# Latent attention in a two-layer decoder trunk: queries and keys of a head left on the partitions of their product, and pair projections kept apart

## The chip, the core and the metric

The kernel runs on one core of one Trainium2 chip. The metric is the device time of one execution in microseconds (us). Five engines matter: TensorE (PE, matmuls; PEld is its weight load), VectorE (DVE), ScalarE (ACT), GpSimd (POOL), and SyncE (SP), whose queue issues every DMA of this kernel. Matmuls write into PSUM, from where only ACT and DVE read the results; SBUF holds everything else, on 128 partitions.

## The reference

Two layers, each with four gated branches on the same input (512 positions, 1024 channels): RWKV-7 time mixing, multi-head latent attention, a causal depthwise convolution of width 31, and cross-attention into 256 memory tokens. The branches are projected, merged by gates, projected once more, and normalised. The change lies in latent attention, with 8 heads, 64 dimensions without and 32 with rotation:

```python
def _mla_branch(q_lat, kv_lat, k_pe, gate, cos, sin, q_norm, w_uq, kv_norm, w_ukv):
    q = (_rms_norm(q_lat, q_norm) @ w_uq).reshape(B, S, H, MLA_NOPE + MLA_ROPE)
    kv = (_rms_norm(kv_lat, kv_norm) @ w_ukv).reshape(B, S, H, MLA_NOPE + MLA_V)
    ...
    q_full = jnp.concatenate([q_nope, q_pe], axis=-1)
    k_full = jnp.concatenate(
        [k_nope, jnp.broadcast_to(k_pe[:, :, None, :], (B, S, H, MLA_ROPE))], axis=-1)
    o = _causal_block_attention(q_full, k_full, v, (MLA_NOPE + MLA_ROPE) ** -0.5)
    return o.reshape(B, S, BRANCH_WIDTH) * jax.nn.silu(gate)
```

A second place is RWKV's token shift, `p = p + mu * (p_prev - p)`, which mixes each position with the one before it.

## The kernel before, in words

**Precision.** Every fp32 operand of a projection is split in two parts, h (a rounded cast) and l (the rest). A product is three matmuls: h by l, h by h, l by h (`mm3`). So a projection of 128 channels by 512 positions over 1024 input channels is 24 matmuls of 128x512 (`project`).

**Order of the work.** The program is straight-line, and Python decides its order while building it. A class `Plan` (L67) keeps an estimated clock for each engine. The main stream (`stream`, L1860) yields the projections' matmuls one after another; everything else (evacuations, softmax steps, convolution taps) is a generator that was spawned as a task with a due time. `Plan.run` (L147) takes the task that is due first if its time has come on PE's clock, and otherwise the next piece of the stream. A task that yields the word "slack" is due no earlier than DVE's clock. The order so found is the order of the instructions on each engine; the waits between engines are added from the data they share.

**Weights.** `stream` works on a list of items. `pick` chooses the first item that is ready; `prefetch` starts the weight DMAs of up to four half-blocks ahead into two raw buffers; `weights` (L435) spawns the split of each, a cast on ACT and a subtraction on DVE. So at any time casts of coming weights (names like w24h) stand in ACT's queue between the evacuations.

**PSUM.** The pool "pp" has two buffers for projections, "pa" has two, "pg" has four for attention. A projection's first matmul waits until the buffer of the one before the last has been read out.

**A pair of heads.** Latent attention goes by four pairs per layer. `pair_item` (L1416) takes one block of weights, issues the DMAs that put the rotated rows of the queries (qrh, qrl) into rows 64 to 96 of the head's tiles qT and qTl, and then has 9 matmuls for the queries of two heads (pq) and 6 for their keys (pk), each into one buffer of "pp". In a product head 0 lies on partitions 0 to 64 and head 1 on 64 to 128. `heads` (L1441) evacuates it: one ACT operation writes the h part xqh or xkh, one DVE operation the l part xql or xkl, both on 128 partitions, into staging tiles; then four DMAs of half a tile each bring the heads' rows to rows 0 to 64 of qT, qTl, kTh and kTl. A head's score matmuls (`mla_block`, L1471: ms) use rows 0 to 96. After the softmax, mt transposes the probabilities and mo multiplies them with the values.

**Other work in the same stretch.** The projections xq of cross-attention (ps_xq), its scores and products (xs, xt, xo, with the transposed probabilities xPTh and xPTl), gates (ps_mg, ps_xg), and the convolution's 31 taps per channel block on DVE (cacc), which fill DVE between the rest.

Of the kernel before, what the change touches and what calls it, by code (L numbers as in the profile page):

```python
# [21 lines left out]
LAYERS = 2  # L22
SEQ = 512
DM = 1024
U_SLOTS = 32
ORDER = ["z0", "m0", "m1", "z2", "m2", "m4", "z3", "m3", "m5"]
LOOK = 4
GATHER = 1500.0
# [38 lines left out]
class Plan:  # L67
# [79 lines left out]
    def run(self, stream):  # L147

        blocked, over, last = None, False, 0.0
        while True:
            now = self.now()
            for task in self.tasks:
                if callable(task[2]) and task[2]():
                    task[0], task[2] = max(task[0], now), None
                elif task[2] == "slack":
                    task[0] = max(task[0], self.clk["DVE"])
            if self.cut != (128, 128):
                last = now  # L160
            wait = last + GATHER if self.cut == (128, 128) and not over else 0.0
            due = min((x for x in self.tasks if not callable(x[2])),
                      key=lambda x: max(x[0], wait) if x[2] == "small" else x[0], default=None)
            at = due and (max(due[0], wait) if due[2] == "small" else due[0])
            if blocked == "pe" or callable(blocked) and blocked() or isinstance(blocked, float) and blocked <= now:
                blocked = None
            if due is not None and at <= now:
                self._step(due)
            elif blocked is None and not over:
                self.t = now  # L170
                try:
                    blocked = next(stream)
                except StopIteration:
                    over = True
            else:
                times = [due[0]] if due is not None else []
                if isinstance(blocked, float):
                    times.append(blocked)
                if times:
                    last = 0.0  # L180
                    self.clk["PE"] = max(now, min(times))
# [84 lines left out]
def trunk_kernel(ctx: ExitStack, tc: tile.TileContext, A, out, dbg=None):  # L266
# [87 lines left out]
    tsh = cp.tile([128, 512], F32, tag="tsh", name="tsh")  # L354
    G.memset(tsh[:, 0:1], 0.0)
# [242 lines left out]
    def layer_items(l):  # L598
        items = []
# [3 lines left out]
        def pr(n, i=0, w=1):  # L603
            return PRM[l][0][:, PCOL[n] + i:PCOL[n] + i + w]
# [5 lines left out]
                return PRM[l][1][:, c:c + 1]  # L610
            return PRM[l][0][:, PCOL[n] + i:PCOL[n] + i + 1]

        def item(blocks, run, ready=None, picked=None, soon=None):
            items.append((blocks, run, ready, picked, soon))

        def ch_item(i, name, after, ready=None, picked=None):

# [62 lines left out]
            plan.spawn(parts())  # L680

        def mix(i, ps, dst):
            S.activation(tsh[:, 1:512], ps[:, 0:511], AF.Copy, scale=pr("mu", i))
            V.scalar_tensor_tensor(out=dst, in0=ps, scalar=PRM[l][2][:, i:i + 1], in1=tsh, op0=ALU.mult, op1=ALU.add)

        def wlal(ps):
            x = u("lora" + t_)
# [435 lines left out]
        def taps(i, hpad):  # L1123
            a = u(f"cacc{i}" + t_)
            V.tensor_scalar(out=a, in0=hpad[:, 0:512], scalar1=hp("conv_w", 31 * i), scalar2=pr("conv_b", i), op0=ALU.mult, op1=ALU.add)
            yield
            for k in range(1, 31):
                V.scalar_tensor_tensor(out=a, in0=hpad[:, k:k + 512], scalar=hp("conv_w", 31 * i + k), in1=a, op0=ALU.mult, op1=ALU.add)
                L["taps"][i] = k
                yield "slack"  # L1130
            cacc[i] = a
            L["nacc"] += 1
            if L["nacc"] == 4:
                yield from conv_norm()

        def conv_norm():
# [18 lines left out]
            for i in range(4):  # L1155
                ps, = yield from pa.take([128, 512], f"cb{i}" + t_)
                plan.due(*ntok)
                yield "pe"
                for tb in range(4):
                    TR(ps[:, 128 * tb:128 * tb + 128], ntok[tb][:, 128 * i:128 * i + 128])  # L1160
                yield
                t, z = u(f"ctn{i}" + t_), u(f"yc{i}" + t_)
# [95 lines left out]
        def lat_item(nb):  # L1258
            def run(get):
# [14 lines left out]
                if nb == 0:  # L1274
# [7 lines left out]
                    L["kT"] = [tuple(m(f"kT{n}{i}" + t_, 512, f"kT{n}{i}", 1, 96, F32R) for n in "hl") for i in range(4)]  # L1282
# [16 lines left out]
        def key_rotary():  # L1299
# [13 lines left out]
            pa.free()  # L1313
            plan.due(*kr)
            yield
            for kT in L["kT"]:
# [77 lines left out]
        def query_rotary(qp):  # L1394
# [9 lines left out]
            for g in range(2):  # L1404
# [8 lines left out]
                pa.free()  # L1413
                qpe.append(t)

        def pair_item(hh):  # L1416
            def run(get):
                wq = yield from get()
                wk = yield from get()
                there = []  # L1420
                qT = [(m(f"qT{hh}{h}" + t_, 512, "lq", 4, 96, F32R),
                       m(f"qTl{hh}{h}" + t_, 512, "qo", 1, 96, F32R) if hh % 2 > h else
                       u(f"qTl{hh}{h}" + t_, 512, F32R, 96) if hh % 2 else m(f"qTl{hh}{h}" + t_, 512, "qp", 2, 96, F32R)) for h in range(2)]
                kT = [L["kT"][2 * (hh % 2) + h] for h in range(2)]
                for h in range(2):
                    r = 64 * (hh % 2) + 32 * h
                    for x, y in zip(qT[h], qpe[hh // 2]):
                        DMA(x[64:96].bitcast(F32), y[r:r + 32].bitcast(F32), f"qTpe{hh}{h}" + t_)
                for w, ks, T, n, s in ((wq, range(3), qT, "q", MSCALE), (wk, range(3, 5), kT, "k", 1.0)):
                    ps = pp.tile([128, 512], F32, tag="pp", name=f"p{n}{hh}" + t_)  # L1430
                    for i, k in enumerate(ks):
# [4 lines left out]
                    plan.spawn(heads(T, ps, n, s, there))  # L1436
                plan.spawn(pair(hh, qT, kT, there))
            item([(A["w_qk"][l, hh], (384, 256))], run,
                 lambda: len(latT) == 5 and len(qpe) > hh // 2 and len(vtok) == 4 and L["pairs"] >= hh - 1 and MEM[l] is not None)

        def heads(T, ps, n, s, there):  # L1441

            parts = [u(f"x{n}{x}" + t_, 512, F32R) for x in "hl"]
            S.activation(parts[0], ps, AF.Copy, scale=s)
            V.scalar_tensor_tensor(out=parts[1], in0=ps, scalar=s, in1=parts[0].bitcast(F32), op0=ALU.mult, op1=ALU.subtract)
            plan.due(*parts)
            yield
            for i, x in enumerate(parts):
                for h in range(2):
                    y = T[h][i]  # L1450
                    DMA(y[0:64].bitcast(F32), x[HALF[h]].bitcast(F32), f"{n}{i}{h}" + y.tensor.name)
                    there.append(f"{n}{i}{h}" + y.tensor.name)

        def pair(hh, qT, kT, there):
            yield lambda: L["turn"] == hh and len(there) == 8
            mo, = yield from pg.take([128, 512], f"mo{hh}" + t_)
            plan.t = max(plan.t, *(plan.done[x][0] for x in there + [f"qTpe{hh}1" + t_]))
            yield
            left = [2]
            for i in range(4):  # L1460
# [10 lines left out]
        def mla_block(hh, h, i, T, mo, two, done, left):  # L1471
# [388 lines left out]
    def stream(items):  # L1860


        items, todo, held, runs = list(items), [], [], []
        count, look = [0], [3]

        def pick():
            for n, (blocks, run, ready, _, _) in enumerate(items):
# [6 lines left out]
            for n, (blocks, run, ready, _, soon) in enumerate(items):  # L1874
                if soon and soon():
                    return n
            return None

        def prefetch():
            while len(held) < look[0] + (0 if items else 2) and wlive["raw"] < WR:  # L1880
                if not todo:
                    n = pick()
                    if n is None:
                        return
                    blocks, run, _, picked, _ = items.pop(n)
                    if picked:
                        picked()
                    todo.extend(blocks)
# [133 lines left out]
```

## Time and profile before

| | |
|---|---|
| median of 3 runs | 1520.82 us (1518.16 to 1522.56) |
| the profiled execution's own time | 1519.87 us |
| its span in the trace | 1518.1 us |
| mean granted clock of PE | 0.997 |
| PE busy | 1485.7 us, 98% |
| DVE, ACT, POOL busy | 71%, 45%, 9% |
| DMA traffic | 153.54 MB, mean 101 GB/s |

Rows of the page and of the trace name a group of instructions by line, engine, operation and tile, such as "L235 ACT ACTIVATE xqh<-pq 128x512". Line 235 is the wrapper through which all ACT, DVE and POOL operations go, 286 that of matmuls, 291 that of transposes, 298 that of DMAs, so tiles tell more than lines. "x8 | 4.8, 598" means eight instructions, 4.8 us busy in all, 598 ns each. What stands in brackets, or behind the second bar, is idle time of that engine just before, and what ended it.

### The profile page before, as it was taken

What the parts mean: (1) busy time and instruction counts of PE and PEld (TensorE: products, weight loads), DVE (VectorE), ACT (ScalarE), POOL (GpSimd) and SP (SyncE); (2) the same over time, 40 slices, a digit from 0 to 9 for tenths busy, and PEclk for the clock granted to TensorE, in tenths of its full rate; (3) what the DMA queues carried; (4) which work ended last, traced back from release to release, by engine and by line L of the source; (5) the groups of instructions that cost most, each with busy time, mean ns of one, the idle gap of its engine ahead of it and who ended that gap; (6) DMA issues with size and microseconds to landing.
All of it is one profiled execution on the core that took longest, in us unless ns stands there. A gap on an engine that the chain in (4) does not pass through costs nothing.

```text
span 1518.1 us, 29700 instructions
## 1 busy us (share of the span) xinstructions
PE 1485.7 (98%) x11896; PEld 1238.0 (82%) x11896; DVE 1072.7 (71%) x2231; ACT 686.6 (45%) x1499; POOL 135.8 (9%) x323
## 2 busy tenths in 40 slices
PE   8999999999999999999999999999999999999997
PEld 8877788887887878888999877888887878788886
DVE  5788988765757675555554889997766586756747
ACT  5535653445245453344255556533443545443432
POOL 0000000030402021000010000000030303120002
PEclk9999999999999999999999999999999999999999
DMA  6443333322232323433343252433232323235231
GB/s 211 124 113 93 104 100 98 98 85 83 74 93 60 94 74 93 139 98 114 123 146 114 81 125 69 121 107 97 81 99 61 93 64 93 69 95 181 98 116 65
DMA packets 89018, 153.54 MB, mean 101 GB/s; under 512 B 41008, under 2 KB 47152, under 8 KB 88880
## 3 DMA queue, kind: packets, MB, share of 16 engines
q1 hardware_dynamic: 88880, 151.65, 33.9%
q8 instruction: 93, 1.52, 0.4%
q14 instruction: 45, 0.37, 0.1%
HBM read 134.32 MB, written 5.77 MB: 92 GB/s over the span
## 4 chain that ended last, share of the span: by engine, by line
PE 89%; DVE 5%; DMA 2%; ACT 2%; issue 1%; SPq 1%; POOL 0%; ACTq 0%; DVEq 0%; POOLq 0%
PE ps_m L286 22%; PE po L286 11%; PE ps_cg L286 3%; PE ps_rg L286 3%; PE ps_v L286 3%; PE ps_xg L286 3%; PE ps_mg L286 3%; PE ps_k L286 3%; PE ps_r L286 3%; PE ps_val L286 3%; PE pz L286 2%; PE ms L286 2%; PE pl L286 2%; PE ps_glu L286 2%; PE ps_xq L286 2%; PE x L286 2%
## 5 line engine op out<-in xcount | busy, mean ns | idle before, releaser
L235 DVE SCALAR_TENSOR_TENSOR cacc<-hpad,prm,cacc 128x512 f32<-128x512 f32 x240 | 178.9, 748 | 3.3
L235 ACT ACTIVATE tm<-ps_m,prm 128x512 f32<-128x512 f32 x64 | 44.1, 689 | 148.5 <-PE ps_m L286 134.7
L235 DVE SCALAR_TENSOR_TENSOR mt<-tm,po 128x512 f32<-128x512 f32 x48 | 33.0, 687 | 79.2 <-PE po L286 79.1
L235 POOL TENSOR_SCALAR ZT<-W 64x256 f32<-64x256 f32 x8 | 4.8, 600 | 621.8 <-DMA W<-scr 287.7
L235 POOL TENSOR_TENSOR ZT<-ZT,tmpW 64x14 f32<-64x14 f32 (+6 forms) x112 | 44.0, 393 | 8.8
L235 ACT ACTIVATE mP<-ms,nmm 128x512 f32<-128x512 f32 (+3 forms) x64 | 33.7, 529 | 18.3 <-DVE nmm L235 17.4
L235 POOL TENSOR_TENSOR tmpW<-ZT,W 64x14 f32<-64x14 f32 (+6 forms) x112 | 39.9, 356 | 7.9
L235 ACT COPY mPT<-mt 128x512 f32<-128x512 f32 (+3 forms) x64 | 26.7, 429 | 22.4 <-PE mt L291 17.1
L235 DVE TENSOR_TENSOR merged<-merged,mt 128x512 f32<-128x512 f32 x48 | 33.8, 704 | 1.6
L235 DVE TENSOR_REDUCE nmm<-ms 128x1 f32<-128x512 f32 (+3 forms) x64 | 29.9, 483 | 0.6 <-PE ms L286 0.2
L235 POOL TENSOR_SCALAR gr<-gm 128x8 f32<-128x8 f32 x8 | 2.3, 286 | 311.2 <-DVE gm L235 311.2
L291 PE MATMUL mt<-cst,mP 128*128 128x128 f32 x160 | 27.1, 276 | 2.6 <-DVE mP L235 2.2
L235 DVE SCALAR_TENSOR_TENSOR merged<-tm,po 128x512 f32<-128x512 f32 x16 | 11.0, 687 | 22.0 <-PE po L286 20.3
L235 DVE TENSOR_SCALAR mP<-mP,smm 128x512 f32<-128x512 f32 (+3 forms) x64 | 24.8, 387 | 2.3
L235 ACT ACTIVATE yb<-yb,mr,gr 128x64 f32<-128x64 f32 x64 | 22.1, 430 | 9.0 <-DVE mr L235 9.0
L235 POOL TENSOR_SCALAR lrs<-lmv 128x1 f32<-128x1 f32 x8 | 2.5, 315 | 263.5 <-DVE lmv L235 261.8
L291 PEld LDWEIGHTS mt<-cst,mP 128*128 128x128 f32 x160 | 18.6, 141 | 8.2 <-ACT mo L235 2.2
L235 ACT ACTIVATE z<-z,lnb,lrs 128x256 f32<-128x256 f32 (+1 forms) x16 | 9.6, 647 | 31.2 <-DVE lnb L235 31.2
L286 PE MATMUL ms<-kTl,qT 96*128 96x512 f32 (+3 forms) x64 | 22.2, 347 | 0.0
L286 PE MATMUL mo<-mPT,v 128*64 128x128 f32 x320 | 21.4, 278 | 0.5 <-ACT mPT L235 0.5
L286 PE MATMUL ms<-kTh,qT 96*128 96x512 f32 (+3 forms) x64 | 20.6, 322 | 0.0
L286 PEld LDWEIGHTS mo<-mPT,v 128*64 128x64 f32 x320 | 17.3, 136 | 4.0 <-issue 2.9
(3535 smaller groups left out, 5323.2 us busy)
## 6 DMA issues: line engine op xcount, KB each, us to landing
w<-in_w_ch_dram SPq DMA_DIRECT2D x146, 512.0 KB, 3.6
w<-in_w_o_dram SPq DMA_DIRECT2D x32, 512.0 KB, 3.6
w<-in_w_out_dram SPq DMA_DIRECT2D x16, 512.0 KB, 3.6
w<-in_w_lat_dram SPq DMA_DIRECT2D x16, 336.0 KB, 3.3
w<-in_w_mk_dram SPq DMA_DIRECT2D x8, 512.0 KB, 3.5
w<-in_w_mv_dram SPq DMA_DIRECT2D x8, 512.0 KB, 3.5
w<-in_w_qk_dram SPq DMA_DIRECT2D x8, 320.0 KB, 3.1
x<-in_xT_dram SPq DMA_DIRECT2D x8, 256.0 KB, 5.6
```

The costliest lines, as they stand in the source:

```text
L235: return self.plan.keep(f(*a, **k))
L286: plan.keep(nc.tensor.matmul(o, lhsT, rhs, start=start, stop=stop))
L291: plan.keep(nc.tensor.transpose(o, i, ident))
```

## The change

- `heads` writes each half of a product straight into the head's own tile, on the partitions where the half lies: for each half one ACT operation (h part) and one DVE operation (l part) on 64 partitions, with a yield between the halves. The staging tiles and the copies by DMA are gone, 8 of 128 KB per pair, 64 in all.
- Tiles qT, qTl, kTh, kTl get 128 rows instead of 96. For head 0 of a pair nothing moves. For head 1 the product's rows are 64 to 128, the rotated ones 32 to 64, and rows 0 to 32 are set to zero by POOL; its score matmuls run over 128 rows (`ROPE`, `ROWS`).
- `pair_item` is marked `apart`: `pick` does not take a pair directly behind a pair if another item is ready.
- The convolution's taps yield "idle" instead of "slack", which makes them due one unit after DVE's clock.
- RWKV's `mix` needs no shift tile: ACT writes (1 - mu) times the product into the destination, and DVE adds mu times the product, one position on, in place. The pool of staging tiles has 33 slots instead of 32, and one tile of the convolution's normalisation moved to another pool.

In the order that this gives, layer 0 has pair 0, then a projection of xq, then pair 1 spread among scores; pair 2 is followed by scores and ps_mg, pair 3 by ps_xq. In layer 1 pair 1 comes right behind pair 0, pair 2 is followed by ps_val, and pair 3 is spread. The number of matmuls is the same, 9336 instructions in the program; ACT and DVE get 16 operations more each, POOL 23 more.

```diff
         def mix(i, ps, dst):
-            S.activation(tsh[:, 1:512], ps[:, 0:511], AF.Copy, scale=pr("mu", i))
-            V.scalar_tensor_tensor(out=dst, in0=ps, scalar=PRM[l][2][:, i:i + 1], in1=tsh, op0=ALU.mult, op1=ALU.add)
+            S.activation(dst, ps, AF.Copy, scale=PRM[l][2][:, i:i + 1])
+            V.scalar_tensor_tensor(out=dst[:, 1:512], in0=ps[:, 0:511], scalar=pr("mu", i), in1=dst[:, 1:512], op0=ALU.mult, op1=ALU.add)
...
-                yield "slack"
+                yield "idle"
...
-                    task[0] = max(task[0], self.clk["DVE"])
+                    task[0] = max(task[0], self.clk["DVE"] + (task[2] == "idle"))
...
+                    for i in (1, 3):
+                        for x in L["kT"][i]:
+                            G.memset(x[0:32].bitcast(F32), 0.0)
...
-                    DMA(x[64:96].bitcast(F32), y.bitcast(F32))
+                    DMA(x[ROPE[i % 2]].bitcast(F32), y.bitcast(F32))
...
+        ROPE, ROWS = [slice(64, 96), slice(32, 64)], [slice(0, 96), slice(0, 128)]
...
-                        DMA(x[64:96].bitcast(F32), y[r:r + 32].bitcast(F32), f"qTpe{hh}{h}" + t_)
+                        if h:
+                            G.memset(x[0:32].bitcast(F32), 0.0)
+                        DMA(x[ROPE[h]].bitcast(F32), y[r:r + 32].bitcast(F32), f"qTpe{hh}{h}" + t_)
...
-        def heads(T, ps, n, s, there):
-
-            parts = [u(f"x{n}{x}" + t_, 512, F32R) for x in "hl"]
-            S.activation(parts[0], ps, AF.Copy, scale=s)
-            V.scalar_tensor_tensor(out=parts[1], in0=ps, scalar=s, in1=parts[0].bitcast(F32), op0=ALU.mult, op1=ALU.subtract)
-            plan.due(*parts)
-            yield
-            for i, x in enumerate(parts):
-                for h in range(2):
-                    y = T[h][i]
-                    DMA(y[0:64].bitcast(F32), x[HALF[h]].bitcast(F32), f"{n}{i}{h}" + y.tensor.name)
-                    there.append(f"{n}{i}{h}" + y.tensor.name)
+        def heads(T, ps, s, there):
+
+            for half, (hi, lo) in zip(HALF, T):
+                S.activation(hi[half], ps[half], AF.Copy, scale=s)
+                V.scalar_tensor_tensor(out=lo[half], in0=ps[half], scalar=s, in1=hi.bitcast(F32)[half], op0=ALU.mult, op1=ALU.subtract)
+                there.extend((hi, lo))
+                yield
...
-            mm3(ps, *(x[:, dg] for x in T[0]), *(x[:, 0:n] for x in T[1]), True, False)
+            mm3(ps, *(x[ROWS[h], dg] for x in T[0]), *(x[ROWS[h], 0:n] for x in T[1]), True, False)
...
-                    return n
+                    if not (apart and last[0]):
+                        return n
+                    second = n if second is None else second
+            if second is not None:
+                return second
```

More of the change, by code (lines that the diff above doesn't have):

```diff
@@ L24 @@
 DM = 1024
-U_SLOTS = 32
+U_SLOTS = 33
 ORDER = ["z0", "m0", "m1", "z2", "m2", "m4", "z3", "m3", "m5"]
@@ L156, in run @@
                     task[0], task[2] = max(task[0], now), None
-                elif task[2] == "slack":
-                    task[0] = max(task[0], self.clk["DVE"])
+                elif task[2] in ("slack", "idle"):
+                    task[0] = max(task[0], self.clk["DVE"] + (task[2] == "idle"))
             if self.cut != (128, 128):
@@ L353, in trunk_kernel @@
     G.memset(mhalf, -0.5)
-    tsh = cp.tile([128, 512], F32, tag="tsh", name="tsh")
-    G.memset(tsh[:, 0:1], 0.0)
     hpads = [cp.tile([128, 542], F32, tag=f"hpad{i}", name=f"hpad{i}") for i in range(2)]
@@ L611, in hp, with item @@
             return PRM[l][0][:, PCOL[n] + i:PCOL[n] + i + 1]
-        def item(blocks, run, ready=None, picked=None, soon=None):
-            items.append((blocks, run, ready, picked, soon))
+        def item(blocks, run, ready=None, picked=None, soon=None, apart=False):
+            items.append((blocks, run, ready, picked, soon, apart))
         def ch_item(i, name, after, ready=None, picked=None):
@@ L1161, in conv_norm @@
                 yield
-                t, z = u(f"ctn{i}" + t_), u(f"yc{i}" + t_)
+                t, z = sp.tile([128, 512], F32, tag="tg", name=f"ctn{i}" + t_), u(f"yc{i}" + t_)
                 S.activation(t, ps, AF.Tanh, scale=hp("cln_g", i), bias=hp("cln_b", i))
@@ L1281, in run @@
                     L["kpe"] = m("kpe" + t_, 128, "kpe", 1)
-                    L["kT"] = [tuple(m(f"kT{n}{i}" + t_, 512, f"kT{n}{i}", 1, 96, F32R) for n in "hl") for i in range(4)]
+                    L["kT"] = [tuple(m(f"kT{n}{i}" + t_, 512, f"kT{n}{i}", 1, 128, F32R) for n in "hl") for i in range(4)]
+                    for i in (1, 3):
+                        for x in L["kT"][i]:
+                            G.memset(x[0:32].bitcast(F32), 0.0)
                 for tb in range(4):
@@ L1315, in key_rotary @@
             yield
-            for kT in L["kT"]:
+            for i, kT in enumerate(L["kT"]):
                 for x, y in zip(kT, kr):
-                    DMA(x[64:96].bitcast(F32), y.bitcast(F32))
+                    DMA(x[ROPE[i % 2]].bitcast(F32), y.bitcast(F32))
                 plan.t += 2000.0
@@ L1419, in run @@
                 wk = yield from get()
[L1420 to L1423, printed above, removed]
+                qT = [(m(f"qT{hh}{h}" + t_, 512, "lq", 4, 128, F32R),
+                       m(f"qTl{hh}{h}" + t_, 512, "qo", 1, 128, F32R) if hh % 2 > h else
+                       u(f"qTl{hh}{h}" + t_, 512, F32R) if hh % 2 else m(f"qTl{hh}{h}" + t_, 512, "qp", 2, 128, F32R)) for h in range(2)]
                 kT = [L["kT"][2 * (hh % 2) + h] for h in range(2)]
@@ L1427, in run @@
                     for x, y in zip(qT[h], qpe[hh // 2]):
-                        DMA(x[64:96].bitcast(F32), y[r:r + 32].bitcast(F32), f"qTpe{hh}{h}" + t_)
+                        if h:
+                            G.memset(x[0:32].bitcast(F32), 0.0)
+                        DMA(x[ROPE[h]].bitcast(F32), y[r:r + 32].bitcast(F32), f"qTpe{hh}{h}" + t_)
+                there = []
                 for w, ks, T, n, s in ((wq, range(3), qT, "q", MSCALE), (wk, range(3, 5), kT, "k", 1.0)):
@@ L1435, in run @@
                     free()
-                    plan.spawn(heads(T, ps, n, s, there))
+                    plan.spawn(heads(T, ps, s, there))
                 plan.spawn(pair(hh, qT, kT, there))
             item([(A["w_qk"][l, hh], (384, 256))], run,
-                 lambda: len(latT) == 5 and len(qpe) > hh // 2 and len(vtok) == 4 and L["pairs"] >= hh - 1 and MEM[l] is not None)
-        def heads(T, ps, n, s, there):
-            parts = [u(f"x{n}{x}" + t_, 512, F32R) for x in "hl"]
-            S.activation(parts[0], ps, AF.Copy, scale=s)
-            V.scalar_tensor_tensor(out=parts[1], in0=ps, scalar=s, in1=parts[0].bitcast(F32), op0=ALU.mult, op1=ALU.subtract)
-            plan.due(*parts)
-            yield
-            for i, x in enumerate(parts):
-                for h in range(2):
-                    y = T[h][i]
-                    DMA(y[0:64].bitcast(F32), x[HALF[h]].bitcast(F32), f"{n}{i}{h}" + y.tensor.name)
-                    there.append(f"{n}{i}{h}" + y.tensor.name)
+                 lambda: len(latT) == 5 and len(qpe) > hh // 2 and len(vtok) == 4 and L["pairs"] >= hh - 1 and MEM[l] is not None, apart=True)
+        def heads(T, ps, s, there):
[4 more added lines that the diff above has]
+                yield
         def pair(hh, qT, kT, there):
@@ L1456, in pair @@
             mo, = yield from pg.take([128, 512], f"mo{hh}" + t_)
-            plan.t = max(plan.t, *(plan.done[x][0] for x in there + [f"qTpe{hh}1" + t_]))
+            plan.due(*there)
+            plan.t = max(plan.t, plan.done[f"qTpe{hh}1" + t_][0])
             yield
@@ L1863, in stream @@
         items, todo, held, runs = list(items), [], [], []
-        count, look = [0], [3]
+        count, look, last = [0], [3], [False]
         def pick():
-            for n, (blocks, run, ready, _, _) in enumerate(items):
+            second = None
+            for n, (blocks, run, ready, _, _, apart) in enumerate(items):
                 if not blocks and ready is None:
@@ L1872, in pick @@
                 if ready is None or ready():
-                    return n
-            for n, (blocks, run, ready, _, soon) in enumerate(items):
+                    if not (apart and last[0]):
[3 more added lines that the diff above has]
+                return second
+            for n, (blocks, run, ready, _, soon, _) in enumerate(items):
                 if soon and soon():
@@ L1884, in prefetch @@
                         return
-                    blocks, run, _, picked, _ = items.pop(n)
+                    blocks, run, _, picked, _, last[0] = items.pop(n)
                     if picked:
```

## The prediction, made before the changed kernel ran

> **What bounds the kernel now.** I read the page's head first, then the windows by stage, then the waits of TensorE (PE) in the two stages that the change touches.
>
> ```profile
> span 1518.1 us, 29700 instructions
> ...
> PE 1485.7 (98%) x11896; PEld 1238.0 (82%) x11896; DVE 1072.7 (71%) x2231; ACT 686.6 (45%) x1499; POOL 135.8 (9%) x323
> ```
>
> PE is busy for 98% of the span and the change takes no matmul away, so the time can only move through PE's gaps and its clock. Latent attention lies at about 100 to 236 us in layer 0 and at 860 to 996 us in layer 1. In the windows the columns are the stretch, its length, then busy time of each engine, the granted clock, the DMA share and GB/s:
>
> ```profile
> 100.00:236.00 136.00, 128.23 (x783) 103.20 (x782) 117.34 (x264) 72.37 (x192) 0.00 (x0) 0.99 0.40 104
> 236.00:715.00 479.00, 476.95 (x4314) 389.73 (x4313) 309.60 (x622) 205.47 (x421) 56.89 (x140) 1.00 0.31 93
> ...
> 860.00:996.00 136.00, 133.69 (x820) 108.68 (x819) 122.04 (x270) 76.65 (x195) 0.00 (x0) 1.00 0.37 97
> 996.00:1465.00 469.00, 467.92 (x4272) 381.46 (x4272) 328.19 (x666) 196.51 (x404) 59.34 (x140) 1.00 0.33 97
> ```
>
> PE idles 136 - 128.23 = 7.8 us in the first attention stage and 136 - 133.69 = 2.3 us in the second. The two long stages behind them idle 2.05 and 1.08 us. The waits of PE (waited in total, times, longest) name the idle time, first for layer 0, then for layer 1:
>
> ```profile
> PE pq L286 <- DVE xql L235: 2.8, 1, 2.8
> PE mt L291 <- DVE mP L235: 2.2, 2, 1.8
> PE ps_xq L286 <- DVE xql L235: 1.0, 1, 1.0
> PE xs L286 <- ACT xqh L235: 0.7, 1, 0.7
> PE mo L286 <- ACT mPT L235: 0.5, 1, 0.5
> PE mt L291 <- DVE smm L235: 0.3, 1, 0.3
> PE xs L286 <- DVE xql L235: 0.2, 1, 0.2
> ```
>
> ```profile
> PE xo L286 <- DVE xPTl L235: 2.0, 2, 1.6
> PE ps_xq L286 <- DVE xql L235: 0.2, 1, 0.2
> ```
>
> These are 7.7 + 2.2 = 9.9 us. The largest is a pair's pq that waits for xql, the evacuation of the pair before: both pairs need the two buffers of the pool "pp". Rows of PE (start, duration, then the idle time before it in brackets) show what else that gap costs:
>
> ```profile
> 105.43 0.39 PE L286 MATMUL pk<-lth,w23l 128*128 128x512 f32 x1
> 108.59 0.79 PE L286 MATMUL pq<-ltl,w24h 128*128 128x512 f32 x1 [2.78 <-DVE xql L235]
> ...
> 112.26 0.39 PE L286 MATMUL pk<-ltl,w24h 128*128 128x512 f32 x1
> ...
> 113.42 0.40 PE L286 MATMUL pk<-lth,w24l 128*128 128x512 f32 x1
> 113.84 0.50 PE L286 MATMUL ps_xq<-xl,w25h 128*128 128x512 f32 x1
> ...
> 149.56 0.41 PE L291 MATMUL mt<-cst,mP 128*128 128x128 f32 x2 [1.81 <-DVE mP L235]
> ...
> 162.23 0.50 PE L286 MATMUL ps_xq<-xl,w29h 128*128 128x512 f32 x1 [1.00 <-DVE xql L235]
> ```
>
> ```profile
> 883.83 0.39 PE L286 MATMUL pq<-ltl,w145h 128*128 128x512 f32 x1
> ...
> 885.87 0.39 PE L286 MATMUL pk<-ltl,w145h 128*128 128x512 f32 x1
> ```
>
> ```profile
> 105.00:110.00 5.00, 2.22 (x7) 1.51 (x6) 2.90 (x7) 2.41 (x5) 0.00 (x0) 0.84 0.25 57
> ...
> 150.00:155.00 5.00, 5.00 (x37) 3.86 (x36) 4.92 (x13) 3.68 (x11) 0.00 (x0) 1.00 0.30 76
> ```
>
> Nine pq matmuls take 112.26 - 108.59 = 3.67 us behind the 2.78 us gap and 885.87 - 883.83 = 2.04 us in layer 1: the granted clock fell (0.84), which cost 1.63 us more. Behind the gap of 1.81 us it stayed 1.00. So PE loses 9.9 + 1.6 = 11.5 us in the two stages, and that is what the change can win or add to.
>
> **The change part by part.** (1) Evacuation in halves. Before, one ACT and one DVE operation on 128 rows empty a product; after, two of each on 64 rows. The nearest rows:
>
> ```profile
> L235 ACT ACTIVATE xqh<-pq 128x512 fp32r<-128x512 f32 x8 | 4.8, 598 | 12.7 <-PE pq L286 12.7
> L235 ACT ACTIVATE lora<-lora 64x512 f32<-64x512 f32 x2 | 1.3, 634 | 1.6 <-DVE lora L235 1.6
> ```
>
> ```profile
> L235 DVE SCALAR_TENSOR_TENSOR xql<-pq,xqh 128x512 fp32r<-128x512 f32 x8 | 5.5, 690 | 5.0 <-ACT xqh L235 4.7 <-DMA qTl<-xql 0.3
> L235 DVE TENSOR_TENSOR lxa<-lora,lxa 64x512 fp32r<-64x512 f32 x2 | 1.4, 690 | 0.0
> ```
>
> Half the partitions take the same time: 634 against 598 ns, 690 against 690. So 16 evacuations cost 16 x 0.63 = 10 us more of ACT and 16 x 0.69 = 11 us more of DVE. As throughput this is hidden: DVE has 136 - 117.34 = 18.7 and 136 - 122.04 = 14.0 us free for 5.5 us in each stage; without that cover it would be 5.5 us a layer. As latency it is not. In the built program the first matmul behind a pk waits for the last DVE operation on pq's second half, and ACT's operation on the second half waits for DVE's on the first, since they share a bank. The chain is ACT, DVE, ACT, DVE instead of ACT, DVE. What one chain takes now:
>
> ```profile
> 112.46 0.60 ACT L235 ACTIVATE xqh<-pq 128x512 fp32r<-128x512 f32 x1 [3.65 <-PE pq L286]
> ```
>
> ```profile
> 113.09 0.69 DVE L235 SCALAR_TENSOR_TENSOR xql<-pq,xqh 128x512 fp32r<-128x512 f32 x1 [1.10 <-ACT xqh L235]
> ```
>
> From 112.46 to PE's 113.84 it takes 1.38 us, and six pk matmuls hide it (112.26 to 113.65, 1.4 us; PE idled next to nothing). Two chains take 2.8 us. Also, on ACT the first half of k stands ahead of the second half of q in the built order, and it cannot start before pk ends. From pk's end: that operation 0.5 (they start about 0.5 apart), q's second half 0.6, DVE 0.69 and the steps between, about 0.1 each: 1.9 us of idle at least. There are five such places: pairs 0, 2 and 3 of layer 0 (followed by ps_xq, ps_mg, ps_xq), pairs 0 and 2 of layer 1 (followed by pq1, ps_val).
>
> [...]
>
> What stands ahead on ACT adds to the 1.9. Layer 0, pair 0: the splits of the next two weights stand ahead of q, and in before the second came late:
>
> ```profile
> 103.98 0.51 ACT L235 CAST w24h<-w 128x384 fp32r<-128x384 f32 x1 [0.93 <-DMA w<-in_w_qk_dram]
> 106.39 0.62 ACT L235 CAST w25h<-w 128x512 fp32r<-128x512 f32 x1 [1.90 <-DMA w<-in_w_ch_dram]
> ```
>
> If it lands at 104 PE idles 2.0 us; if at 106.4, with three more casts and q and k behind it, PE resumes at about 110.0, 4.2 us after pk ends, and pays the clock: 5.8. I take the middle, 4.0, against 4.4 before (2.8 + 1.6). Pairs 2 and 3 of layer 0 have a short queue: 1.9 each, against 1.0 and 0. Layer 1, pair 0: now ACT takes q as soon as pq ends,
>
> ```profile
> 886.07 0.60 ACT L235 ACTIVATE xqh<-pq 128x512 fp32r<-128x512 f32 x1 [0.48 <-PE pq L286]
> ```
>
> and after it stand a softmax step, two weight casts and a cast of a gated output before k and q's second half: six at 0.5 us put that half at about 889.1, its DVE operation behind two others at 890.3 or 891.0, pk's end at 887.3. That is 3.0 to 3.7 of idle (2.0 if the casts had been done earlier); I take 3.2, and the clock's 1.6: 4.8. Layer 1, pair 2 has two operations and one DVE split ahead: 1.9 to 2.8, I take 2.5; it lies between 1.81 and 2.78, so half of the clock's cost: 3.3.
>
> (2) The 64 copies of half tiles go, from SP's queue and the DMA engines. The xo waits of layer 1 (2.0) hang on them, since the cast xPTh came late behind a copy, as did its DVE part:
>
> ```profile
> 898.80 0.59 ACT L235 CAST xPTh<-xt 128x512 fp32r<-128x512 f32 x1 [1.56 <-DMA qT<-xqh]
> ```
>
> With the xs waits (0.9) and the 0.2 of ps_xq they go; late next there is the softmax chain that the list names already. The mt and mo waits (2.2 + 0.5 + 0.3 = 3.0) are a softmax chain; I keep them.
>
> (3) Odd heads use 128 rows instead of 96, with 32 zeroed:
>
> ```profile
> L286 PE MATMUL ms<-kTh,qT 96*128 96x512 f32 x16 | 6.3, 395 | 0.0
> ...
> L286 PE MATMUL xo<-xPTh,vmh 128*128 128x512 f32 x16 | 6.2, 391 | 0.0
> ```
>
> The same time. The zeroing is 24 memsets on POOL, the nearest being
>
> ```profile
> L235 POOL MEMSET reset<- 128x256 bf16 x1 | 0.3, 312 | 0.3 <-POOLq L2014 0.3
> ```
>
> 0.3 to 0.6 us each, on an engine that is 0.00 busy in both stages. Rope transfers of the odd heads queue behind one on SP; the rope rows come well before the first ms. Nothing; 0.6 a pair if not covered.
>
> (4) "apart", "idle", the mix with no shift tile, one more slot: order and buffers. They can at most take the 2.05 + 1.08 us idle of the long stages, or add as much: 0.
>
> **Sum.** After: 4.0 + 1.9 + 1.9 + 3.0 + 4.8 + 3.3 = 18.9 us. Before: 11.5. That is +7.4 on the profiled execution's 1519.87 us (span 1518.1 and 1.8 around it), 1527.3; the median of the runs lies 0.95 above that execution, so 1528.2.
>
> **The rivals.** *Slow clock everywhere.* The threshold may lie just under 1.9. Then the two 1.9 places pay 1.6 each, layer 1's pair 2 0.8 more, and if the late weight comes too 1.8 more: 5.8 on top, 1534. For: the 0.84 behind 2.78. Against: 1.00 behind 1.81.
> [...]
>
> *Faster: the second half is done beside pk.* If ACT and DVE are through with both halves within pk's 1.4 us and a little more, each place costs the 1.0 of the 162.23 row (5.0 in all), and if half the softmax waits go with the freed queues, 1.5: 6.5 against 11.5, -5, 1515.8. It decides at q's second half starting on ACT before pk ends. Against: the built order on ACT.
>
> *Exchange.* All five at 1.9 to 2.0 with no clock loss, softmax waits as they are: 9.8 + 3.0 = 12.8, +1.3, about 1522. For: casts that come early in layer 1, as 883 to 886 us had ACT idle.
>
> *The copies were never on the path* (the change doesn't shorten anything): then the 2.0 of xo stays too: 1530.2, within the forecast.
>
> **How the numbers follow.** Forecast (and the last rival) 0.43, slow clock everywhere 0.15, exchange 0.20, faster 0.22. About 0.3% (4.6 us) is what a measurement of this kernel can tell from no change: 1516.3 to 1525.4 is "same". Slower 0.58, same 0.20, faster 0.22. The range runs from 1515 (most of the faster case) to 1535 (slow clock everywhere); the forecast's own is 1522 to 1532, from the ends 2.0 and 5.8, 2.0 and 5.3, 1.9 and 4.4 of its three uncertain places (-6.2 and +3.4 on the sum).
>
> **What would show it.** Right: five gaps of PE behind the last pk of a pair, with DVE's qTl as releaser, of 1.9 us or more; no xo wait on xPTl in layer 1; POOL busy for a few us in both stages; a granted clock under 1 behind the layer 1 pair 0 gap. Wrong: a matmul right behind pk without a gap, or the gaps' sum under 12 us, or a new wait of an ms for a memset or a rope transfer.

## The result, and the profile after

| | median | ratio to before (95% interval) |
|---|---|---|
| before | 1520.42 us (1518.16 to 1522.56) | |
| after | 1538.26 us (1535.39 to 1539.69) | 1.0115 (1.0094 to 1.0136) |

The changed kernel is 17.8 us slower. The forecast was slower too, but by 7.4, and the time lies outside its range. The head of the page of after:

```profile
span 1536.8 us, 29675 instructions
...
PE 1494.7 (97%) x11896; PEld 1245.0 (81%) x11896; DVE 1088.5 (71%) x2247; ACT 696.1 (45%) x1515; POOL 153.4 (10%) x346
```

The span grew by 18.7 us, and PE is busy for 9 us longer with the same matmuls, which take longer at a lower granted clock (mean 0.991 against 0.997): about half of the loss is idle time, about half a slower clock. The waits of PE in after, layer 0 first, then layer 1 (waited in total, times, longest):

```profile
PE ps_xq L286 <- DVE qTl L235: 5.1, 2, 2.6
PE ps_mg L286 <- DVE qTl L235: 2.6, 1, 2.6
PE mt L291 <- ACT xPTh L235: 1.2, 1, 1.2
```

```profile
PE pq L286 <- DVE qTl L235: 3.9, 1, 3.9
PE ps_val L286 <- DVE qTl L235: 3.2, 1, 3.2
PE mo L286 <- ACT mPT L235: 1.0, 2, 0.5
PE ps_xg L286 <- DVE qTl L235: 0.9, 1, 0.9
PE ps_xq L286 <- DVE qTl L235: 0.6, 1, 0.6
PE mt L291 <- DVE mP L235: 0.4, 1, 0.4
```

All five gaps are where they were forecast, released by qTl as forecast, and the xo and xs waits are gone (what took the xo waits away is taken up below). But the two that were put at 1.9 us are 2.6, and there are two small ones more (0.9 and 0.6) behind pairs 3 and 1 of layer 1. Behind every large gap the granted clock falls, to between 0.50 and 0.78 in these windows of after (stretch, length, busy times, then clock, DMA share, GB/s):

```profile
110.00:115.00 5.00, 5.00 (x19) 3.96 (x18) 2.13 (x3) 0.00 (x0) 0.00 (x0) 0.66 0.71 213
```

```profile
164.00:168.00 4.00, 4.00 (x14) 3.25 (x15) 1.40 (x3) 1.18 (x2) 0.00 (x0) 0.62 0.60 175
...
196.00:200.00 4.00, 4.00 (x12) 3.10 (x12) 2.66 (x6) 0.49 (x1) 0.00 (x0) 0.61 0.21 46
```

```profile
896.00:900.00 4.00, 3.73 (x12) 3.28 (x13) 2.18 (x5) 0.00 (x0) 0.00 (x0) 0.50 0.40 131
900.00:905.00 5.00, 4.71 (x23) 3.62 (x21) 2.90 (x7) 2.66 (x7) 0.00 (x0) 0.78 0.09 12
...
960.00:965.00 5.00, 4.94 (x15) 3.94 (x16) 3.44 (x5) 0.00 (x0) 0.00 (x0) 0.66 0.32 102
```

Length times the missing share of the clock gives what PE lost: 1.7, 1.5, 1.6, 2.0 + 1.1 and 1.7 us, 9.6 in all (the windows of 1.5 and 1.6 leave out 0.1 to 0.2 us at their ends).

### The profile page after: what moved, and what is told of

Read it like the earlier page. It is cut to its first block, busy times and chain, and to the rows that moved or that the text cites. A ratio compares the mean times of both kernels' runs of the same rounds, so it can differ in the third digit from the quotient of the medians.

```text
span 1536.8 us, 29675 instructions
## 1 busy us (share of the span) xinstructions
PE 1494.7 (97%) x11896; PEld 1245.0 (81%) x11896; DVE 1088.5 (71%) x2247; ACT 696.1 (45%) x1515; POOL 153.4 (10%) x346
## 4 chain that ended last, share of the span: by engine, by line
PE 88%; DVE 5%; ACT 2%; POOL 1%; DMA 1%; issue 1%; SPq 0%; ACTq 0%; POOLq 0%; DVEq 0%
PE ps_m L286 21%; PE po L286 11%; PE ps_mg L286 3%; PE ps_cg L286 3%; PE ps_rg L286 3%; PE ps_v L286 3%; PE ps_r L286 3%; PE ps_k L286 3%; PE ps_xq L286 3%; PE ps_val L286 3%; PE ps_xg L286 3%; PE ps_glu L286 3%; PE pz L286 2%; PE pl L286 2%; PE ms L286 2%; PE x L286 2%
## 5 line engine op out<-in xcount | busy, mean ns | idle before, releaser
L235 POOL TENSOR_TENSOR ZT<-ZT,tmpW 64x14 f32<-64x14 f32 (+6 forms) x112 | 47.1, 421 | 8.8
L235 POOL TENSOR_TENSOR tmpW<-ZT,W 64x14 f32<-64x14 f32 (+6 forms) x112 | 43.7, 390 | 8.1
L286 PE MATMUL ms<-kTl,qT 96*128 96x256 f32 (+4 forms) x64 | 22.2, 347 | 0.0
L235 ACT ACTIVATE xP<-xs,nmx 128x256 f32<-128x256 f32 x32 | 15.2, 475 | 15.1 <-DVE nmx L235 14.8
L286 PE MATMUL ms<-kTh,qT 96*128 96x256 f32 (+4 forms) x64 | 20.6, 322 | 0.0
```

Of the source, the lines that this page charges most:

```text
L235: return self.plan.keep(f(*a, **k))
L286: plan.keep(nc.tensor.matmul(o, lhsT, rhs, start=start, stop=stop))
```

## The experiments

Each was run beside the kernel before on the same chip; "before" there had medians of 1520.1 to 1521.1.

| run | what it is | median, us | ratio to before (95% interval) |
|---|---|---|---|
| q_whole | after, no yield between the halves | 1533.57 | 1.0090 (1.0071 to 1.0109) |
| h_then_l | after, both h halves, then both l halves | 1528.53 | 1.0045 (1.0026 to 1.0064) |
| stage_dma | after, with one evacuation on 128 rows and copies by DMA | 1514.94 | 0.9965 (0.9950 to 0.9980) |
| stage_pool | the same, copies by POOL | 1516.43 | 0.9974 (0.9965 to 0.9984) |
| stage_mix | the same, h by DMA and l by POOL | 1515.54 | 0.9967 (0.9955 to 0.9980) |
| warm | after, with matmuls that nobody reads in the gaps | 1535.77 | 1.0100 (1.0086 to 1.0115) |
| no_apart | after, pairs not kept apart | 1543.02 | 1.0146 (1.0129 to 1.0163) |
| stage_no_apart | stage_dma, pairs not kept apart | 1511.35 | 0.9941 (0.9929 to 0.9953) |
| stage_pool_no_apart | stage_pool, pairs not kept apart | 1518.66 | 0.9985 (0.9976 to 0.9994) |
| before_idle | before, with "idle" for the taps | 1512.27 | 0.9946 (0.9933 to 0.9960) |
| stage_slack | stage_no_apart, with "slack" | 1519.96 | 0.9995 (0.9984 to 1.0007) |
| halves | after, with "slack", not apart | 1546.84 | 1.0170 (1.0152 to 1.0189) |

**Is it the evacuation in halves, or the order?** stage_dma puts the old evacuation back and keeps everything else of the change:

```diff
-            for half, (hi, lo) in zip(HALF, T):
-                S.activation(hi[half], ps[half], AF.Copy, scale=s)
-                V.scalar_tensor_tensor(out=lo[half], in0=ps[half], scalar=s, in1=hi.bitcast(F32)[half], op0=ALU.mult, op1=ALU.subtract)
-                there.extend((hi, lo))
-                yield
+            parts = [u("xs" + x + t_, 512, F32R) for x in "hl"]
+            S.activation(parts[0], ps, AF.Copy, scale=s)
+            V.scalar_tensor_tensor(out=parts[1], in0=ps, scalar=s, in1=parts[0].bitcast(F32), op0=ALU.mult, op1=ALU.subtract)
+            plan.due(*parts)
+            yield
+            for half, (hi, lo) in zip(HALF, T):
+                for x, y in zip(parts, (hi, lo)):
+                    DMA(y[half].bitcast(F32), x[half].bitcast(F32))
+                there.extend((hi, lo))
```

> Edit: the changed kernel with the evacuation of the kernel before: one ACT and one DVE operation on 128 rows into staging tiles, then four DMAs per product, which now keep the partitions; rows, zeroing, the spacing of pairs and all other edits stay as changed. Theory A: the gaps behind pk fall to 0 to 1 us, except layer 0's pair 0 (weights' casts ahead, 1 to 2.8 us); 1517 to 1522, as before. Rival B (the spacing of pairs and the new order cost the time): 1533 or more. Rival D (128 rows and the zeroing cost): 1533 or more too, with waits of ms on POOL or on DMA in the list.

It ran at 1514.94 us, 23.3 under after and 5 under before. Its waits behind a pk (released by the staging tile xsl), layer 0 and layer 1:

```profile
PE ps_mg L286 <- DVE xsl L235: 0.4, 1, 0.4
PE ps_xq L286 <- DVE xsl L235: 0.4, 1, 0.4
PE ps_glu L286 <- DVE xsl L235: 0.3, 1, 0.3
```

```profile
PE pq L286 <- DVE xsl L235: 0.6, 1, 0.6
...
PE ps_xq L286 <- DVE xsl L235: 0.2, 1, 0.2
```

Gaps of 2.6 to 3.9 have become 0.2 to 0.6. So the halves cost the time; 128 rows, zeroing and spacing do not (rivals B and D fall; of D's signs there is one wait of ms for a DMA of rotated rows, 0.7 us). The copies were cheap: they come back here, and the kernel is faster than before.

**Which part of the chain?** q_whole takes the yield between the halves out, h_then_l also orders the operations ACT, ACT, DVE, DVE (the lines shown are h_then_l's; q_whole only moves the yield):

```diff
             for half, (hi, lo) in zip(HALF, T):
                 S.activation(hi[half], ps[half], AF.Copy, scale=s)
+            for half, (hi, lo) in zip(HALF, T):
                 V.scalar_tensor_tensor(out=lo[half], in0=ps[half], scalar=s, in1=hi.bitcast(F32)[half], op0=ALU.mult, op1=ALU.subtract)
                 there.extend((hi, lo))
-                yield
+            yield
```

> Edit: in the changed kernel the yield between the two halves of an evacuation goes, so that both halves of q stand ahead of k's on ACT and DVE. Theory A (the added time is the five gaps behind a pair's last pk and the halved clock behind each): the chain of four operations starts at pq's end instead of waiting for k's first half, about 3.0 us of which pk hides 1.4, so a gap falls from 2.6 to about 1.6 us where ACT's queue is short, under the 1.81 us after which the clock stayed full; 1.0 and 1.6 us less at each of five places, about 13 us less than the changed kernel's 1538: near 1525. Rival B (the added time is the new order of items and tasks): near 1538. Rival C (the gaps matter, the clock does not recover): 5 us less, 1533.

> Edit: both halves of h by ACT first, then both halves of l by DVE, q ahead of k; only one handover between the engines. Theory A: the chain is 0.6 + 0.6 + 0.7 + 0.7 = 2.6 us and 1.4 of it lie beside pk: gaps of about 1.2 us, full clock, 1523. If ACT and DVE wait for one another whenever they read one bank, this and q_whole differ by the handovers alone (0.2 to 0.4 us a place, 1 to 2 us in all). Rival B (order): near 1538.

1533.6 and 1528.5: each step takes back about 5 us, not 13 and 15. The waits of layer 0, q_whole and then h_then_l:

```profile
PE ps_xq L286 <- DVE qTl L235: 5.7, 3, 2.1
PE ps_mg L286 <- DVE qTl L235: 1.5, 1, 1.5
```

```profile
PE ps_xq L286 <- DVE qTl L235: 3.4, 2, 1.9
PE ps_xq L286 <- ACT kTh L235: 2.3, 1, 2.3
PE ps_mg L286 <- DVE qTl L235: 1.4, 1, 1.4
```

At the place with a short queue (ps_mg, pair 2) the gap fell as expected, 2.6 to 1.5 and 1.4. Elsewhere gaps of about 2 us stay, and a projection behind pair 1 waits in both, where after had none. Four short operations in a row were too long for six pk matmuls in all three orders tried; and with other costs the planner also makes another order, so these two are not after with one thing less. That q_whole landed on rival C's 1533 is luck: C had smaller gaps and a clock that stays low, and the trace has the reverse. From first pq to pz of both layers PE idles 22.0 us, against 22.3 in after, while the granted clock of the run rose from 0.991 to 0.996. In h_then_l both got better: 19.0 us of idle time, clock 0.995.

**What does the clock cost?** warm adds 11 matmuls that nobody reads behind the five pairs.

```diff
                 plan.spawn(pair(hh, qT, kT, there))
+                if (l, hh) in ((0, 0), (0, 2), (0, 3), (1, 0), (1, 2)):
+                    d, = yield from pg.take([128, 512], f"dum{hh}" + t_)
+                    for i in range(11):
+                        plan.keep(nc.tensor.matmul(d, latT[0][0][:, 0:128], latT[0][0], start=i == 0, stop=i == 10))
+                    pg.free()
```

> Edit: the changed kernel with 11 matmuls of 128x512 more behind the last pk of the five pairs whose gaps cost most, into a buffer of their own that nobody reads, 11 x 0.227 = 2.5 us each; they add work only. Theory A (gap and halved clock are two separate costs, about 15 us and 8 to 9 us): PE stays busy through the gap, its next real matmul comes when it came before, and the clock stays 1.00 behind it, 1.6 us a place and about 3.0 behind the longest gap (3.95 us, of which 1.4 stay open): 8 us less, 1530. Rival C (the clock's loss is not caused by the gap, or costs nothing): 1538. Rival F (the added matmuls delay the real ones): up to 12 us more, 1550.

1535.8, only 2.5 less. But PE's rows in warm show the expected thing at the place itself:

```profile
105.60 0.39 PE L286 MATMUL pk<-lth,w23l 128*128 128x512 f32 x1
105.82 2.65 PE L1448 MATMUL dum<-lth 128*128 128x512 f32 x11
108.39 0.47 PE L286 MATMUL ps_xq<-xl,w24h 128*128 128x512 f32 x1
108.70 0.39 PE L286 MATMUL ps_xq<-xh,w24h 128*128 128x512 f32 x1
108.93 0.39 PE L286 MATMUL ps_xq<-xh,w24l 128*128 128x512 f32 x1
```

The next real matmul starts when the evacuation lets it, 0.15 us behind the end of the qTl operation as in after, and 2.79 us behind the start of the last pk (in after 2.95, 106.64 to 109.59), and the ones behind it start 0.23 us apart; in after they are 0.43 us apart. The granted clock of the whole run is 0.997 against after's 0.991. From layer 0's first pq to its pz, warm takes 611.6 us and after 616.6: 5.0 less, which is the three losses of 1.7, 1.5 and 1.6. In layer 1 it takes 595.5 against 593.5, and waits of warm there, of pair 3 and of the later RWKV stage, say why:

```profile
PE ps_xg L286 <- DVE qTl L235: 3.0, 1, 3.0
```

```profile
PE x L286 <- DVE PT L235: 2.8, 2, 2.5
```

after has 0.9 at the first and no such row at the second. The take of a buffer seems to have moved the order there. So for layer 0 gap and clock are shown to be separate costs; in layer 1 the clock stayed up as well (1.00 from 860 to 1010 us, where after has 0.97), but the new waits took that gain away, and what the clock alone cost there rests on the windows above.

**Spacing of pairs, and the taps' rule.** no_apart and stage_no_apart take out one mark, `apart=True`; before_idle and stage_slack change the taps' rule alone (stage_slack the other way round, and before_idle with the line of `Plan.run` that knows the word):

```diff
-                 ... and MEM[l] is not None, apart=True)
+                 ... and MEM[l] is not None)
```

```diff
-                yield "slack"
+                yield "idle"
```

> Edit: the changed kernel without the mark that keeps pairs apart; the evacuation in halves stays. In layer 1 the order is the same as with it; in layer 0 the first matmuls of pair 1 stand behind pair 0's keys. Theory A: the same gaps of 2.6 us or more behind pk; 1536 to 1541. Rival B (spacing the pairs is what costs): 1530 or less.

> Edit: stage_dma without the mark that keeps pairs apart, so that the projection of pair 1 comes right behind pair 0's in layer 0, as in the kernel before. If spacing the pairs is a gain of its own, the gap of 2.78 us and the halved clock of the kernel before come back at that place and the time is 3 to 5 us over stage_dma's 1514.9: 1518 to 1520. If the gain of stage_dma over the kernel before lies in the other edits (taps, mix, rows), it stays at 1515.

> Edit: the kernel before with one edit of the change alone, the convolution's taps due one unit behind DVE's clock (idle instead of slack). The order of its pair projections becomes that of stage_no_apart (pair 1 behind pair 0 in both layers, pair 3 near pair 2 in layer 1). If the 8.8 us by which stage_no_apart beats the kernel before come from this edit, 1511 to 1514; if they come from the rows that stay on their partitions or from the mix without a shift tile, 1518 to 1522.

> Edit: stage_no_apart with slack again for the taps. Its order is that of the kernel before. If the taps' rule is what gains, 1518 to 1522, with the gap of 2.8 us and its halved clock behind pair 0's pk again; if the rows and the mix gain, 1511 to 1514.

With the halves, spacing gains 4.8 us (1543.0 to 1538.3; no_apart lies 2 us above its expectation); with one evacuation on 128 rows it costs 3.6 (1511.35 to 1514.94), against what was expected. The order itself is neither good nor bad here: it seems to decide whose gap stands where, which these runs do not show in more detail. With copies by POOL it is the other way again:

> Edit: stage_pool (one evacuation on 128 rows, copies on POOL, partitions kept) without the spacing of pairs. Spacing cost 3.6 us with copies by DMA (1514.9 against 1511.4); if that is the order of the items and not the copies, 1511 to 1514 here against stage_pool's 1516.4.

1518.7 against stage_pool's 1516.4: here the spacing gains 2.2, and the expectation was wrong; why is open. It also means that without the spacing the copies by POOL are 7.3 us slower than those by DMA (1518.66 against 1511.35).

The taps' rule is a clear gain: before_idle has the kernel before with the taps' rule changed and runs at 1512.3, 8.8 us faster; stage_slack takes the word back and loses 8.6 (1511.35 to 1519.96). Its time is the expected one, but not by the expected gap: pair 0's is 1.7 us with the clock full behind it, and the clock fell behind a wait of xs (1.45) and one of mt (1.81; mean 0.97 from 97 to 250 us). In layer 0 the waits of before_idle are

```profile
PE pq L286 <- DVE xql L235: 1.8, 1, 1.8
PE xs L286 <- ACT xqh L235: 0.7, 1, 0.7
PE xs L286 <- DVE xql L235: 0.2, 1, 0.2
```

2.7 us instead of 7.7: the wait of mt for mP (2.2) and that of ps_xq for xql (1.0) are gone, and pq's fell from 2.8 to 1.8. All of what its profiled execution gains lies in layer 0 (first pq to pz 606.9 against 612.9 us; layer 1 has 580.5 against 580.0). That execution, 1515.28, is the slowest of five and shows 4.6 of the 8.8 us; the rest is not located.

**Copies on POOL.** In stage_pool all four copies of a product are POOL operations, in stage_mix those of the l parts (the lines shown are stage_pool's, against stage_dma).

```diff
-                    DMA(y[half].bitcast(F32), x[half].bitcast(F32))
+                    G.tensor_copy(out=y[half], in_=x[half].bitcast(F32))
+                    yield
```

> Edit: as stage_dma, but the four copies of a product, which keep the partitions, are POOL operations on 64x512 instead of DMAs. Theory A: the same gaps as stage_dma; POOL is idle there and takes perhaps 1 us for a copy, 4 us for a product, ahead of the scores by more than that except for the first pair of a layer; 1515 to 1522. If a POOL copy takes over 2 us or slows DVE's operations beside it, waits of ms on POOL come and the time goes over 1525. Rival B: 1533 or more.

> Edit: as stage_dma, but only the h parts are copied by DMA and the l parts by POOL. Both copies of a product then go side by side, two DMAs and two POOL operations instead of four of one kind. Theory A: PE's gaps behind pk stay under 1 us, scores can start a little earlier; 1512 to 1517, no more than 0.2% from stage_dma. If POOL operations slow DVE beside them, 1517 to 1520.

1516.4 and 1515.5 against 1514.9: nearly as good, so with the pairs kept apart the carrier of the copies matters little. Without the spacing it was 7.3 us, as said above. The 1 us that was expected of a POOL copy of 64x512 was the author's estimate; the nearest row of before is an operation of POOL on 64x256, ZT<-W, with a mean of 0.60 us.

**The halves alone.**

> Edit: the changed kernel with slack for the taps and without the spacing of pairs, so that of the change there remain the evacuation in halves with its rows and zeroing, and the mix. If the edits add up, it is stage_slack (1520.0) plus the price of the halves as no_apart against stage_no_apart has it (1543.0 - 1511.4 = 31.7): 1552. If the price depends on the order, which puts other work behind pk here and there, it is as after against stage_dma (23.3): 1543.

1546.8, between the two: 26.9 us over stage_slack. The price of the halves is 27 us in the old order with "slack", 32 with "idle", 23 with "idle" and spacing. The whole change is therefore about +27 (halves), -4 ("idle", 1546.8 to 1543.0) and -5 (spacing), together +18 over stage_slack, which runs as before does.

stage_no_apart (1511.35) and before_idle (1512.3) are both faster than both kernels; between the two these runs show no difference that can be told.

## Why the prediction was right or wrong, point by point

- **What bounds the kernel.** Right: PE's gaps and clock in the two stages carry the loss. By stage, first pq of layer 0 to its pz grew by 3.7 us and the same stretch of layer 1 by 13.5 (580.0 to 593.5).
- **The mechanism, a chain ACT, DVE, ACT, DVE at five places.** Right, by place, releaser and experiment: putting back one evacuation takes 23 us off. The handover in the middle shows too: in after, ACT's operation on k's second half starts 0.03 us behind the end of DVE's on the first (at 108.75, 894.83 and 958.62 us), and at 972.88 the trace names DVE's qTl as what q's second half waited for. The two read one buffer, and no run puts them in two, so the wait is shown and its reason is not.
- **The least gap of 1.9 us.** This is the step that failed first: it came out at 2.6, and the gaps put at 3.2 and 2.5 in layer 1 at 3.95 and 3.2. Its terms were 0.5, 0.6, 0.69 and one step of 0.1, though the chain has three steps between operations, and nothing for what stands ahead where ACT's queue is short. Rows at layer 0's pair 2 in after, PE, ACT, DVE:

```profile
160.96 0.39 PE L286 MATMUL pk<-lth,w28l 128*128 128x512 f32 x1
163.96 0.47 PE L286 MATMUL ps_mg<-xl,w29h 128*128 128x512 f32 x1 [2.61 <-DVE qTl L235]
```

```profile
161.39 0.59 ACT L235 ACTIVATE kTh<-pk 64x512 fp32r<-64x512 f32 x1
162.00 0.59 ACT L235 ACTIVATE qT<-pq 64x512 fp32r<-64x512 f32 x1
162.62 0.41 ACT L235 CAST w31h<-w 128x256 fp32r<-128x256 f32 x1
```

```profile
161.94 0.55 DVE L235 TENSOR_TENSOR w31l<-w,w31h 128x384 fp32r<-128x384 f32 x1
162.41 0.68 DVE L235 SCALAR_TENSOR_TENSOR kTl<-pk,kTh 64x512 fp32r<-64x512 f32 x1
163.12 0.69 DVE L235 SCALAR_TENSOR_TENSOR qTl<-pq,qT 64x512 fp32r<-64x512 f32 x1
163.85 0.43 DVE L235 TENSOR_TENSOR w31l<-w,w31h 128x256 fp32r<-128x256 f32 x1
```

  qT is there at 162.59, but DVE is at kTl until 163.09: 0.5 us. kTl is late because a weight split, w31l, stands ahead of it: kTh was there at 161.98. At pair 3, with a gap of 2.56, the weight split stands on ACT instead:

```profile
192.67 0.39 PE L286 MATMUL pk<-lth,w31l 128*128 128x512 f32 x1
```

```profile
192.93 0.61 ACT L235 CAST w34h<-w 128x512 fp32r<-128x512 f32 x1
193.44 0.59 ACT L235 ACTIVATE kTh<-pk 64x512 fp32r<-64x512 f32 x1
194.05 0.59 ACT L235 ACTIVATE qT<-pq 64x512 fp32r<-64x512 f32 x1
```

  The last pk ends at 193.06 and kTh starts 0.38 later; there DVE takes qTl 0.13 us behind qT. Pair 0 has the same 0.39 on ACT. So by these rows about 0.4 of the missing 0.7 us at each place of layer 0 is one split of coming weights ahead of k's first half, on ACT or on DVE. Another 0.1 is the distance of ACT's two starts, 0.61 where the sum had 0.5, and the rest is the steps that were not counted (0.13 and 0.15 at pair 3).
- **The clock.** The second term that failed. The two places at 1.9 were put at no loss, because the clock had stayed full behind one gap of 1.81; at 2.6 each paid 1.5 to 1.6. Layer 1's pair 0 paid 3.1 instead of 1.6, pair 2 1.7 instead of 0.8. The rival of a slow clock everywhere had this effect and its time, 1534, was nearer; but its cause, a threshold just under 1.9, is not what the traces show. In the attention stages of all traces the clock fell behind 17 of the 18 gaps of 2.3 us or more and behind 6 of the 20 between 1.4 and 2.2: here the odds rose with the length, and 1.9 was not safe either.
- **By place**, idle and clock: 4.3 (forecast 4.0), 4.1 (1.9), 4.2 (1.9), 7.0 (4.8), 4.9 (3.3), softmax waits 2.6 (3.0), and the two small gaps 1.5 (0): 28.6 against 18.9. Less before's 11.5 that is +17.1 of the span's 18.7; the stretch ahead of the first pq adds 1.2 (it takes 102.2 to 103.6 us in the traces).
- **Copies off the queue.** The xo waits of layer 1 (2.0) went, but that it was the copies is not shown: before_idle and stage_dma keep the copies by DMA and have no xo wait there either, halves has neither copies nor the wait, and stage_slack, with copies and "slack", has 1.2. Either edit seems to be enough, so the 2.0 came out right without its reason being shown.
- **128 rows and zeroing at nothing.** Not measured alone, but stage_slack, which has both, stands 0.9995 (0.9984 to 1.0007) to before.
- **Part (4) at 0.** Wrong: "idle" is worth 8.8 us in the kernel before and 4 with the halves, and the spacing another 5 with the halves. Its bound, the 3.1 us that the long stages idle, looked at the wrong stage: taps also run in the attention stages, where DVE is 117 of 136 us busy. This error had the other sign and hid part of the first two: the halves by themselves cost 27 us, against 7.4 forecast for the whole change.

## What to carry to other kernels

An evacuation's cost is its latency where the buffer is wanted next, and here an operation on half the partitions took as long as one on all (0.59 against 0.598 us on ACT, 0.68 against 0.69 on DVE): cutting one into two doubled the chain. Cost such a chain on every engine that it passes, with what stands ahead in each queue and every step between; here 0.7 us that the sum left out made gaps of 2.6 us out of 1.9, behind which PE's clock fell (0.61 to 0.66 in the windows of layer 0), and the price doubled. Before dismissing a small scheduling edit, run it alone: one word about who goes first on DVE was worth 8.8 us, and no run here shows a cost of the DMA copies that the change set out to save.

## What the runs showed of the hardware that was not expected

The length of a gap alone did not decide the clock. Behind 1.81 us in before it stayed full, as the prediction showed (1.00 from 150 to 155 us); before_idle has a gap of 1.82, and there it fell, 1.5 us after PE had resumed (mean 0.68 from 108.3 to 113 us; the starts stand 0.23 us apart at first and 0.43 apart from 110.09 on):

```profile
108.57 0.50 PE L286 MATMUL pq<-ltl,w24h 128*128 128x512 f32 x1 [1.82 <-DVE xql L235]
...
109.60 0.39 PE L286 MATMUL pq<-lth,w24h 128*128 128x512 f32 x1
109.83 0.46 PE L286 MATMUL pq<-lth,w24l 128*128 128x512 f32 x1
110.09 0.63 PE L286 MATMUL pq<-ltl,w24h 128*128 128x512 f32 x1
```

In q_whole a gap of 2.0 us at 182 us left it at 1.00, and in warm even one of 3.0:

```profile
966.59 0.47 PE L286 MATMUL ps_xg<-xl,w154h 128*128 128x512 f32 x1 [3.04 <-DVE qTl L235]
966.89 0.40 PE L286 MATMUL ps_xg<-xh,w154h 128*128 128x512 f32 x1
967.12 0.40 PE L286 MATMUL ps_xg<-xh,w154l 128*128 128x512 f32 x1
```

The wait of mt for mP is 1.81 us in before and in stage_slack, and only in stage_slack did the clock fall behind it. The loss, where there is one, did not follow the length closely either. In windows of 1 us from PE's return it is 1.7 us behind 1.81 (stage_slack), 2.3 (h_then_l), 2.6 and 3.2 us (after) alike, which is about 3.4 us at half clock (0.50 in the window of after from 896 us); but it is 3.0 behind 3.95 in after and 3.1 behind another gap of 3.2 in no_apart. What decides whether and when the clock falls is not shown.

In after, operations on a second half, which start on partition 64, did not overlap their neighbours: the DVE rows above, 0.68 and 0.69 us long, start 0.71 and 0.73 us apart, where whole ones of 0.68 us start 0.60 apart (890.99 and 891.59 in after), about 0.1 us more a step. ACT shows the same: around its second halves of 0.59 us the starts stand 0.61 and 0.62 us apart in the rows above, instead of 0.49 (106.11 and 106.60 in after, a first half and the cast behind it). The reason is not shown.
